# The latent adaLN sums of a diffusion block: three engines' shares against one chain on VectorE

## The chip, the core and the metric

The program runs on one core of one Trainium2 chip. A core has five engines that work side by side, each through its own instructions in order: TensorE (PE in the profile, with its weight loads as PEld), VectorE (DVE), ScalarE (ACT), GpSimd (POOL) and SyncE (SP), which here issues nearly all transfers from HBM. The metric is the device time of one execution in microseconds; less is better. The time before is 1447.01 us, the median of three runs (1440.1 to 1449.32).

## The reference, cut to what matters

One transformer block for 256 latent tokens (width 2048) and 256 context tokens: adaLN, neighbourhood attention with 16 heads, output projection, ConvFFN.

```python
sh1, sc1, g1, sh2, sc2, g2 = adaln(cond_lat, w_ada[i], b_ada[i])    # silu(c) @ w + b, split in six
h = modulate(rms_norm(x, norm_mix_g[i]), sh1, sc1)
csh1, csc1, ... = adaln(cond_ctx, w_ada[i], b_ada[i])
hc = modulate(rms_norm(ctx, norm_mix_g[i]), csh1, csc1)
y, yc = neighbourhood_attention(h, hc, ...)                         # w_qkv, softmax over 256+256 keys, w_o
x = x + g1 * y
hf = modulate(rms_norm(x, norm_ffn_g[i]), sh2, sc2)
x = x + g2 * conv_ffn(hf, ...)
```

The change touches one piece of this: the latent vectors g1, sh2, sc2 and g2. Each is a product of one vector of 2048 values with a 2048 x 2048 part of `w_ada`, thus 2048 x 2048 weights read for 2048 results.

## The kernel before, in words

**Stages.** The products with `w_qkv` come in twelve groups of 512 output columns. For head group 0 (k) and head groups 0 and 1 (v) they are computed at the start, piece by piece, while the first part of adaLN (shift and scale of the mixer) comes in. Then, for each group of four heads (groups 0 to 3), `project` computes the next products: with four token tiles of 128 for k and v (`nt` = 4, latent and context tokens), with two for q (`nt` = 2). In order of time these are q0; k, q of group 1; v, k, q of group 2; k, q, v of group 3. Between the matmuls of such a product the attention of the group before is woven in. Then come the output projection (`w_o`, five rounds in the table `WO`), a norm, the ConvFFN with `w_up` (22 products) and `w_down` (5).

**The split of weights.** Each product is made of three fp32r products of high and low parts. For each weight tile pair (256 x 512 values, 512 KB) SyncE loads `wr`, ScalarE writes the high part `wh` (line 155), VectorE the low part `wl` (line 156). There are four `wr` slots, three of `wh` and two of `wl`, and `ahead` issues two pairs ahead.

**The latent adaLN sums.** `ada_tasks` (lines 252 to 301) makes one column of 512 results out of eight tiles `wa` (each two k of 128 x 512 values); there are 12 columns ahead of the FFN (g1, then sh2, then gs2) and 4 in it (g2). Every k is one step: multiply by the value of the condition that belongs to the row, and add to `acc`. Of the eight parts of a column, three (q = 0, 3, 6) are a chain of multiply-adds on VectorE (lines 274 and 279); the other five are multiplied on ScalarE in place (line 276) and added on GpSimd (line 277) to a second accumulator, whose first step is on VectorE. `finish` adds the two accumulators on VectorE (line 285), transposes on TensorE (line 288), reduces (line 291) and adds the bias (line 294). There are three slots of `wa` (`WA`), and each part starts with the issue of a load two parts ahead, which waits until the part before has let go of its slot.

**What sets the order.** The program is written as one stream of instructions, and a scheduler sets the order on each engine from it. The stream is paced by credits: `ada.tick(r)` adds r, and each whole credit takes one part off the queue. Before, `project` adds 0.44 x `nt` for each weight pair: 1.76 parts with four token tiles, 0.88 with two; in the output projection it is one part for each weight pair, in the FFN 0.25. Attention is paced in the same way by `side.tick`, once for each token tile in `nat` (line 381).

**The normalisation chain.** At the end of a head group, q and k are normalised and transposed (`norm_transpose`, line 515): ScalarE squares (521), VectorE scales (522), GpSimd takes a power (195), VectorE does a Newton step in three instructions of 128 x 4 values (196, 197, 200) and a multiply (526), TensorE transposes (532), ScalarE and VectorE split the result (534, 535). The attention of the next group waits for it.

Of the kernel before, what the change touches and what calls it, by code (L numbers as in the profile page):

```python
# [9 lines left out]
F32 = mybir.dt.float32  # L10
# [5 lines left out]
P = 128  # L16
# [9 lines left out]
CH = 512  # L26
# [3 lines left out]

WA = 3
EPS = 1e-6
# [18 lines left out]
def block_kernel(  # L51
# [200 lines left out]
    def ada_tasks(pool, i, c, dst, gcol=None):  # L252
# [3 lines left out]


        st = {}
# [4 lines left out]
        def part(q):  # L263
            w, pool_ = st[q], q % 3 != 0
            if q < 2:
                st["acc", pool_] = pool.tile(
                    [P, CH], F32, tag=f"acc{pool_}", name="acc", bufs=2 - pool_
                )
            acc = st["acc", pool_]
            for k in range(KT):  # L270
                s = sT[:, q * KT + k, 0:1]
                first = q < 2 and k == 0
                if first:
                    nc.vector.tensor_scalar_mul(acc, w[:, k, :], s)
                elif pool_:
                    nc.scalar.mul(w[:, k, :], w[:, k, :], s)  # L276
                    nc.gpsimd.tensor_add(acc, acc, w[:, k, :])  # L277
                else:
                    nc.vector.scalar_tensor_tensor(  # L279
                        out=acc, in0=w[:, k, :], scalar=s, in1=acc, op0=ALU.mult, op1=ALU.add  # L280
                    )

        def finish():
            acc = st["acc", 0]
            nc.vector.tensor_add(acc, acc, st["acc", 1])
            sp = ms()
# [83 lines left out]
    def nat(psl, tt0, w, kt0, n, first, last):  # L370

        wh, wl = w
        for i, pt in enumerate(psl):
            ts = slice((tt0 + i) * P, (tt0 + i + 1) * P)
            for k in range(n):
# [4 lines left out]
                nc.tensor.matmul(pt, hl(kt, ts), wh[:, k, :], start=False, stop=z)  # L380
            side.tick(side.rate)

    def project(c0, nt):
        psl = [pj() for _ in range(nt)]
        for kt in range(0, KD, KT):
            nat(psl, 0, weight(w_qkv, kt, KT, c0, CH), kt, KT, kt == 0, kt == KD - KT)
            ada.tick(0.44 * nt)
        return psl
# [278 lines left out]

    cols = [ada_tasks(ap, 2, c, g1T) for c in range(4)]
    cols += [ada_tasks(ap, 3, c, sh2T) for c in range(4)]
    cols += [ada_tasks(ap, 4, c, gs2T, S_GF) for c in range(4)]  # L670
    ada.extend(ada_pieces(cols))

# [90 lines left out]
    for i, pieces in enumerate(WO):  # L763
# [5 lines left out]
        for c, cn, k_lo, k_hi in pieces:  # L769
            tick = (lambda: side.tick(cn / 340)) if i == 0 else (lambda: ada.tick(1.0))  # L770
            proj(w_o, NH, c, cn, omv, tick, k_lo, k_hi, pts[c], fold)
# [187 lines left out]
```

## Time and profile before

| | |
|---|---|
| time, median of 3 | 1447.01 us |
| profiled execution: its time, its span | 1445.85 us, 1444.0 us |
| TensorE busy | 1399.1 us (97%) |
| VectorE, ScalarE, GpSimd busy | 1000.0, 778.5, 281.1 us |
| adds on GpSimd (line 277) | 144, 1553 ns on average |
| scalings on ScalarE (line 276) | 144, 718 ns on average |
| multiply-adds on VectorE (line 279) | 80, 921 ns on average |

The span is from the first to the last instruction; 1.85 us of the profiled execution's time lie outside of it. PE is nearly always busy, so time can be found only where PE waits, where its clock was granted at less than full speed, or where an engine beside it begins to make it wait. The profile shows each of these by stage.

### The profile page before, as it was taken

What the parts mean: (1) busy time and instruction counts of PE and PEld (TensorE: products, weight loads), DVE (VectorE), ACT (ScalarE), POOL (GpSimd) and SP (SyncE); (2) the same over time, 40 slices, a digit from 0 to 9 for tenths busy, and PEclk for the clock granted to TensorE, in tenths of its full rate; (3) what the DMA queues carried; (4) which work ended last, traced back from release to release, by engine and by line L of the source; (5) the groups of instructions that cost most, each with busy time, mean ns of one, the idle gap of its engine ahead of it and who ended that gap; (6) DMA issues with size and microseconds to landing.
All of it is one profiled execution on the core that took longest, in us unless ns stands there. A gap on an engine that the chain in (4) does not pass through costs nothing.

```text
span 1444.0 us, 21091 instructions
## 1 busy us (share of the span) xinstructions
PE 1399.1 (97%) x7608; PEld 1167.8 (81%) x7608; DVE 1000.0 (69%) x1541; ACT 778.5 (54%) x1356; POOL 281.1 (19%) x208
## 2 busy tenths in 40 slices
PE   5999999999999999999899999999999999999998
PEld 2666787877787887888788888888888888888888
DVE  4556687686868768756768787887877775545454
ACT  4322265775555675755556566665666654333333
POOL 1000025465445555300101111111111000000000
PEclk9999999999999999999899999999999999999999
DMA  9999548687677677545567777777776666566554
GB/s 308 357 333 313 190 125 269 206 259 218 214 219 254 215 239 232 178 138 189 174 201 224 237 230 242 236 229 234 228 240 196 182 175 206 182 207 204 172 173 156
DMA packets 208920, 317.14 MB, mean 220 GB/s; under 512 B 23360, under 2 KB 87744, under 8 KB 208816
## 3 DMA queue, kind: packets, MB, share of 16 engines
q1 hardware_dynamic: 208688, 315.79, 70.4%
q8 instruction: 59, 0.97, 0.3%
q14 instruction: 45, 0.37, 0.1%
q10 hardware_dynamic: 128, 0.01, 0.0%
HBM read 312.75 MB, written 3.01 MB: 219 GB/s over the span
## 4 chain that ended last, share of the span: by engine, by line
PE 74%; issue 9%; DMA 5%; DVE 4%; ACT 3%; POOL 2%; SPq 1%; DVEq 0%; POOLq 0%; ACTq 0%
PE pj L727 18%; PE pj L733 9%; PE mx L727 8%; PE ms L727 7%; PE pj L379 5%; PE pj L378 5%; PE pj L380 5%; PE mx L733 4%; PE ms L733 4%; DMA wa<-in_w_ada 3%; PE ms L411 2%; PE mx L378 2%; PE mx L379 2%; PE mx L380 2%; POOL acc L277 2%
## 5 line engine op out<-in xcount | busy, mean ns | idle before, releaser
L156 DVE TENSOR_TENSOR wl<-wr,wh 128x1024 fp32r<-128x1024 f32 (+2 forms) x425 | 503.8, 1186 | 280.6 <-PE pj L733 106.3
L155 ACT CAST wh<-wr 128x1024 fp32r<-128x1024 f32 (+2 forms) x425 | 412.1, 971 | 428.8 <-PE pj L727 135.1
L277 POOL TENSOR_TENSOR acc<-acc,wa 128x512 f32<-128x512 f32 x144 | 223.6, 1553 | 428.8 <-issue 260.1
L379 PE MATMUL pj<-wl,hh 128*128 128x512 f32 x512 | 204.7, 400 | 3.5 <-DVE wl L156 3.4
L380 PE MATMUL pj<-wh,hl 128*128 128x512 f32 x512 | 201.7, 397 | 0.0
L378 PE MATMUL pj<-wh,hh 128*128 128x512 f32 x512 | 194.4, 400 | 2.5 <-ACT hh L450 2.5
L727 PE MATMUL pj<-hf,wh 128*128 128x512 f32 x688 | 176.3, 396 | 2.0 <-DVE hf L819 2.0
L727 PEld LDWEIGHTS pj<-hf,wh 128*128 128x128 f32 x688 | 124.9, 191 | 25.1 <-DVE hf L819 2.8
L276 ACT ACTIVATE wa<-wa,sT 128x512 f32<-128x512 f32 x144 | 97.4, 718 | 74.5 <-DMA wa<-in_w_ada 69.3
L379 PEld LDWEIGHTS pj<-wl,hh 128*128 128x128 f32 x512 | 97.7, 191 | 27.2 <-DVE wl L156 6.3
L378 PEld LDWEIGHTS pj<-wh,hh 128*128 128x128 f32 x512 | 96.8, 190 | 26.9 <-issue 3.4
L380 PEld LDWEIGHTS pj<-wh,hl 128*128 128x128 f32 x512 | 97.5, 191 | 19.5
L733 PEld LDWEIGHTS pj<-hf,wl 128*128 128x128 f32 x688 | 94.6, 192 | 6.8
L733 PE MATMUL pj<-hf,wl 128*128 128x256 f32 x688 | 97.8, 285 | 0.0
L727 PE MATMUL mx<-hf,wh 128*128 128x512 f32 x352 | 97.7, 394 | 0.0
L727 PE MATMUL ms<-hf,wh 128*128 128x512 f32 x336 | 90.9, 390 | 0.0
L279 DVE SCALAR_TENSOR_TENSOR acc<-wa,sT,acc 128x512 f32<-128x512 f32 x80 | 73.7, 921 | 6.9 <-DMA wa<-in_w_ada 6.3
L727 PEld LDWEIGHTS ms<-hf,wh 128*128 128x128 f32 x336 | 63.1, 188 | 14.2
L727 PEld LDWEIGHTS mx<-hf,wh 128*128 128x128 f32 x352 | 60.6, 190 | 7.8
L478 DVE TENSOR_TENSOR vsum<-vsum,mx 128x512 f32<-128x512 f32 x64 | 43.2, 684 | 34.2 <-PE mx L380 34.0
L733 PEld LDWEIGHTS mx<-hf,wl 128*128 128x128 f32 x352 | 53.7, 189 | 7.1 <-DVE wl L156 0.4
L584 POOL TENSOR_TENSOR bt<-bt,maskt 128x384 f32<-128x384 f32 x16 | 17.9, 1123 | 206.4 <-DMA bt<-rpd 173.7
(251 smaller groups left out, 2212.0 us busy)
## 6 DMA issues: line engine op xcount, KB each, us to landing
wr<-in_w_up SPq DMA_DIRECT2D x160, 512.0 KB, 4.5
wa<-in_w_ada SPq DMA_DIRECT2D x128, 512.0 KB, 4.6
wr<-in_w_qkv SPq DMA_DIRECT2D x93, 512.0 KB, 4.8
wr<-in_w_down SPq DMA_DIRECT2D x63, 512.0 KB, 4.8
wx<-in_w_ada SPq DMA_DIRECT2D x56, 512.0 KB, 8.6
wr<-in_w_o SPq DMA_DIRECT2D x24, 512.0 KB, 3.9
wr<-in_w_down SPq DMA_DIRECT2D x45, 256.0 KB, 3.0
wr<-in_w_up SPq DMA_DIRECT2D x16, 384.0 KB, 3.4
```

The source lines that it names most:

```text
L155: a = nc.scalar.copy(hi[:, :kn, :cn], w[:, :kn, :cn])
L156: b = nc.vector.tensor_tensor(out=lo[:, :kn, :cn], in0=w[:, :kn, :cn], in1=hi[:, :kn, :cn].bitcast(F32), op=ALU.subtract,)
L276: nc.scalar.mul(w[:, k, :], w[:, k, :], s)
L277: nc.gpsimd.tensor_add(acc, acc, w[:, k, :])
L279: nc.vector.scalar_tensor_tensor(out=acc, in0=w[:, k, :], scalar=s, in1=acc, op0=ALU.mult, op1=ALU.add)
L378: nc.tensor.matmul(pt, hh[:, kt, ts], wh[:, k, :], start=a, stop=False)
L379: nc.tensor.matmul(pt, hh[:, kt, ts], wl[:, k, :], start=False, stop=False)
L380: nc.tensor.matmul(pt, hl(kt, ts), wh[:, k, :], start=False, stop=z)
L411: nc.tensor.matmul(ap_[32 * k : 32 * k + 32, :n], s32[:, 4 * q + k, :], w[:, k * n : (k + 1) * n], start=(q == 0), stop=(q == 3), tile_pos ...
L478: nc.vector.tensor_add(acc[:, h0 + i, :], acc[:, h0 + i, :], pr_[i])
L727: nc.tensor.matmul(pts[b][:, : t1 - t0], wh[:, k, bs], mov(kt, slice(t0, t1)), start=(kt == 0 and t0 == 0), stop=False,)
L733: nc.tensor.matmul(pts[b][:, :T], wl[:, k, bs], mov(kt, slice(0, T)), start=False, stop=(kt == kn - 1),)
```

## The change

Every part of a column becomes a chain on VectorE: one multiply, then 15 multiply-adds into one accumulator. The scalings on ScalarE, the additions on GpSimd, the second accumulator and the addition in `finish` go. `wa` gets a fourth slot, so that loads are issued three parts ahead. The pace is set for each token tile in `nat` in place of each weight pair: 0.5 with four token tiles and 0.1 with two, thus 2.0 and 0.2 parts for each weight pair (before 1.76 and 0.88). In the output projection it is 0.6 for each weight pair (before 1.0), in the FFN 0.25 as before. The columns of gs2 now come ahead of those of sh2.

```diff
--- before.py
+++ after.py
@@ -28,7 +28,9 @@
 
 RATE, RATE3 = 0.46, 0.36
 
-WA = 3
+ADA_RATE = {2: 0.1, 4: 0.5}
+
+WA = 4
 EPS = 1e-6
 NEG = -1e30
 
@@ -254,35 +256,27 @@
         st = {}
 
         def load(q):
             st[q] = wload(w_ada, q * KT, KT, i * D + c * CH, CH, pool)
 
         def part(q):
-            w, pool_ = st[q], q % 3 != 0
-            if q < 2:
-                st["acc", pool_] = pool.tile(
-                    [P, CH], F32, tag=f"acc{pool_}", name="acc", bufs=2 - pool_
-                )
-            acc = st["acc", pool_]
+            w = st[q]
+            if q == 0:
+                st["acc"] = pool.tile([P, CH], F32, tag="acc", name="acc", bufs=2)
+            acc = st["acc"]
             for k in range(KT):
                 s = sT[:, q * KT + k, 0:1]
-                first = q < 2 and k == 0
-                if first:
+                if q == 0 and k == 0:
                     nc.vector.tensor_scalar_mul(acc, w[:, k, :], s)
-                elif pool_:
-                    nc.scalar.mul(w[:, k, :], w[:, k, :], s)
-                    nc.gpsimd.tensor_add(acc, acc, w[:, k, :])
                 else:
                     nc.vector.scalar_tensor_tensor(
                         out=acc, in0=w[:, k, :], scalar=s, in1=acc, op0=ALU.mult, op1=ALU.add
                     )
 
         def finish():
-            acc = st["acc", 0]
-            nc.vector.tensor_add(acc, acc, st["acc", 1])
+            acc = st["acc"]
             sp = ms()
             for b in range(4):
                 nc.tensor.transpose(sp[:, b * P : (b + 1) * P], acc[:, b * P : (b + 1) * P], ident)
@@ -379,12 +373,14 @@
                 nc.tensor.matmul(pt, hh[:, kt, ts], wl[:, k, :], start=False, stop=False)
                 nc.tensor.matmul(pt, hl(kt, ts), wh[:, k, :], start=False, stop=z)
             side.tick(side.rate)
+            ada.tick(ada.rate)
 
     def project(c0, nt):
         psl = [pj() for _ in range(nt)]
+        ada.rate = ADA_RATE[nt]
         for kt in range(0, KD, KT):
             nat(psl, 0, weight(w_qkv, kt, KT, c0, CH), kt, KT, kt == 0, kt == KD - KT)
-            ada.tick(0.44 * nt)
+        ada.rate = 0.0
         return psl
 
 
@@ -666,8 +662,8 @@
         return [seq + w[0] + s[2] + w[1] + t[2] + s[3] + w[2] + t[3] + w[3]]
 
     cols = [ada_tasks(ap, 2, c, g1T) for c in range(4)]
+    cols += [ada_tasks(ap, 4, c, gs2T, S_GF) for c in range(4)]
     cols += [ada_tasks(ap, 3, c, sh2T) for c in range(4)]
-    cols += [ada_tasks(ap, 4, c, gs2T, S_GF) for c in range(4)]
     ada.extend(ada_pieces(cols))
 
     v, v1 = [[split_v([vsums[g][:, tt, :] for tt in range(4)], g)] for g in range(2)]
@@ -767,7 +763,7 @@
         elif i > 1:
             pts = {c: [bank() for _ in range(cn // P)] for c, cn, _, _ in pieces}
         for c, cn, k_lo, k_hi in pieces:
-            tick = (lambda: side.tick(cn / 340)) if i == 0 else (lambda: ada.tick(1.0))
+            tick = (lambda: side.tick(cn / 340)) if i == 0 else (lambda: ada.tick(0.6))
             proj(w_o, NH, c, cn, omv, tick, k_lo, k_hi, pts[c], fold)
         if i == 0:
             side.drain()
```

In the changed kernel's rows below, lines have moved: 156 is 158, 279 is 274, 274 is 272, 291 is 285, 196, 197 and 200 are 198, 199 and 202, 522 and 526 are 518 and 522, 788 is 784.

The first place is VectorE's order in the product for k of head group 2 (the groups are 0 to 3; four token tiles), over two weight pairs. `acc` and `wa` are the adaLN sums, `wl` the low part of a weight pair, `rs` and `ptl` belong to attention. Before:

```order
L156 TENSOR_TENSOR wl<-wr,wh 128x1024
L279 SCALAR_TENSOR_TENSOR acc<-wa,sT,acc 128x512
L623 RECIPROCAL rs<-rs 128x1
L291 TENSOR_REDUCE sh2T<-ms 128x4
L279 SCALAR_TENSOR_TENSOR acc<-wa,sT,acc 128x512
L294 TENSOR_TENSOR sh2T<-sh2T,sm 128x4
L156 TENSOR_TENSOR wl<-wr,wh 128x1024
L279 SCALAR_TENSOR_TENSOR acc<-wa,sT,acc 128x512 x2
L636 TENSOR_TENSOR ptl<-ms,pth 128x4x128 x2
L285 TENSOR_TENSOR acc<-acc 128x512
```

And now:

```order
L158 TENSOR_TENSOR wl<-wr,wh 128x1024
L274 SCALAR_TENSOR_TENSOR acc<-wa,sT,acc 128x512
L619 RECIPROCAL rs<-rs 128x1
L274 SCALAR_TENSOR_TENSOR acc<-wa,sT,acc 128x512
L619 RECIPROCAL rs<-rs 128x1
L274 SCALAR_TENSOR_TENSOR acc<-wa,sT,acc 128x512 x2
L285 TENSOR_REDUCE g1T<-ms 128x4
L288 TENSOR_TENSOR g1T<-g1T,sm 128x4
L158 TENSOR_TENSOR wl<-wr,wh 128x1024
L274 SCALAR_TENSOR_TENSOR acc<-wa,sT,acc 128x512
L272 TENSOR_SCALAR acc<-wa,sT 128x512
L274 SCALAR_TENSOR_TENSOR acc<-wa,sT,acc 128x512 x2
```

Each weight pair now has four steps of the sums where it had two; over the eight pairs of this product they are 32 where they were 12.

The second place is VectorE's order in the product for q that follows (two token tiles), where the normalisation chains of the group's end lie (`ss`, `nt`, `nr`, `qn`). Before:

```order
L156 TENSOR_TENSOR wl<-wr,wh 128x1024
L274 TENSOR_SCALAR acc<-wa,sT 128x512
L526 TENSOR_TENSOR qn<-oT,nr 128x512
L522 TENSOR_SCALAR ss<-ss 128x4
L279 SCALAR_TENSOR_TENSOR acc<-wa,sT,acc 128x512
L291 TENSOR_REDUCE sh2T<-ms 128x4
L156 TENSOR_TENSOR wl<-wr,wh 128x1024
L274 TENSOR_SCALAR acc<-wa,sT 128x512
L196 TENSOR_TENSOR nt<-nr 128x4
L294 TENSOR_TENSOR sh2T<-sh2T,sm 128x4
L522 TENSOR_SCALAR ss<-ss 128x4
L197 SCALAR_TENSOR_TENSOR nt<-nt,ss 128x4
```

And now:

```order
L158 TENSOR_TENSOR wl<-wr,wh 128x1024
L202 SCALAR_TENSOR_TENSOR nr<-nt,nr 128x4
L198 TENSOR_TENSOR nt<-nr 128x4
L522 TENSOR_TENSOR qn<-oT,nr 128x512
L199 SCALAR_TENSOR_TENSOR nt<-nt,ss 128x4
L202 SCALAR_TENSOR_TENSOR nr<-nt,nr 128x4
L522 TENSOR_TENSOR qn<-oT,nr 128x512
L158 TENSOR_TENSOR wl<-wr,wh 128x1024
L518 TENSOR_SCALAR ss<-ss 128x4
L158 TENSOR_TENSOR wl<-wr,wh 128x1024
L198 TENSOR_TENSOR nt<-nr 128x4
L199 SCALAR_TENSOR_TENSOR nt<-nt,ss 128x4
```

The steps of the sums that stood between the instructions of the chain are gone from here; over the eight pairs of this product they are 6 where they were 7, and 4 of the 6 stand in the first pair.

The third place is VectorE's order in the fourth round of the output projection, where `sacc` gathers the squares for the norm. Before:

```order
L156 TENSOR_TENSOR wl<-wr,wh 128x1024
L788 TENSOR_TENSOR sacc_5379<-sacc_5379,sq 128x256
L156 TENSOR_TENSOR wl<-wr,wh 128x1024
L788 TENSOR_TENSOR sacc_5379<-sacc_5379,sq 128x256 x2
L156 TENSOR_TENSOR wl<-wr,wh 128x1024 x4
```

And now:

```order
L158 TENSOR_TENSOR wl<-wr,wh 128x1024
L274 SCALAR_TENSOR_TENSOR acc<-wa,sT,acc 128x512
L784 TENSOR_TENSOR sacc_5198<-sacc_5198,sq 128x256
L158 TENSOR_TENSOR wl<-wr,wh 128x1024
L274 SCALAR_TENSOR_TENSOR acc<-wa,sT,acc 128x512
L285 TENSOR_REDUCE sh2T<-ms 128x4
```

About one step of the sums for each weight pair is new here; before, the sums had ended ahead of the output projection.

## The prediction

> **What bounds the kernel now.** The page's first part, and then the view of the stretches: first products end near 195 us, attention with its products runs to 610, the output projection to 705, then a turn and the FFN.
>
> ```profile
> span 1444.0 us, 21091 instructions
> PE 1399.1 (97%) x7608; PEld 1167.8 (81%) x7608; DVE 1000.0 (69%) x1541; ACT 778.5 (54%) x1356; POOL 281.1 (19%) x208
> 195.00:610.00 415.00, 398.85 (x1917) 327.37 (x1916) 314.96 (x481) 262.25 (x548) 207.40 (x143) 0.99 0.72 225
> 610.00:705.00 95.00, 92.76 (x577) 82.50 (x575) 60.44 (x99) 50.14 (x86) 0.00 (x0) 1.00 0.51 165
> 740.00:1130.00 390.00, 390.00 (x2241) 342.83 (x2240) 316.73 (x458) 244.96 (x387) 56.93 (x36) 1.00 0.75 227
> ```
>
> Columns of a stretch: its length, then busy time of PE, PEld, DVE, ACT and POOL, granted clock, DMA share, GB/s. In the FFN stretch PE is busy for all of 390 us although DVE is at 316.73 (81%) and POOL still adds: nothing is to be had there. In the attention stretch PE idles 415 - 398.85 = 16.15 us. That, and time at a lower clock, is all that the change can reach. Some of its products next, one by one:
>
> ```profile
> 376.00:429.00 53.00, 52.45 (x262) 43.77 (x261) 37.14 (x47) 33.27 (x68) 24.76 (x19) 1.00 0.74 226
> 429.00:460.00 31.00, 27.81 (x118) 22.00 (x117) 27.35 (x40) 19.63 (x44) 17.75 (x13) 0.89 0.76 248
> 515.00:543.00 28.00, 28.00 (x146) 23.60 (x145) 21.65 (x35) 20.38 (x57) 13.31 (x10) 1.00 0.79 245
> 543.00:602.00 59.00, 55.28 (x256) 44.81 (x255) 43.35 (x76) 36.53 (x76) 31.17 (x21) 0.97 0.73 224
> ```
>
> The first is the product for k of group 2, the second its q with the normalisation of that group, the third q of group 3, the fourth v of group 3 with its normalisation. PE is full in the first and third (0.55 and 0 us idle) and waits in the second and fourth (3.19 and 3.72 us). The loss sits where the normalisation chains are, not where most of the sums are. These stretches are also those with a clock under 1: (1 - 0.89) x 31 = 3.4 us and (1 - 0.97) x 59 = 1.8 us, together 5.2. Whom PE waits for in 195 to 610 us (us in total, times, longest):
>
> ```profile
> PE pj L379 <- DVE wl L156: 3.4, 4, 1.5
> PE ms L532 <- DVE qn L526: 2.7, 2, 1.5
> PE mx L532 <- DVE qn L526: 2.5, 2, 1.7
> PE mx L645 <- ACT pth L635: 2.1, 1, 2.1
> PE ms L631 <- ACT pr L624: 1.4, 2, 0.8
> PE ms L532 <- ACT kh L534: 1.3, 1, 1.3
> PE ms L532 <- DVE gs2T L291: 0.8, 1, 0.8
> PE pj L727 <- DVE om L566: 0.8, 1, 0.8
> PE ms L648 <- DVE ptl L636: 0.7, 1, 0.7
> ```
>
> Together 15.7 us. What makes DVE and ACT late there? First DVE's groups of this stretch (count, busy us, mean ns), and below the line the same kinds from stretches with little or no work on GpSimd: the first 195 us, and 740 to 1130 us.
>
> ```profile
> L156 DVE TENSOR_TENSOR wl<-wr,wh 128x1024 fp32r<-128x1024 f32 x76 | 106.9, 1407 | 21.0 <-PE pj L379 13.6 <-ACT oT L653 2.9 <-ACT wa L276 1.5
> L279 DVE SCALAR_TENSOR_TENSOR acc<-wa,sT,acc 128x512 f32<-128x512 f32 x60 | 58.7, 979 | 6.8 <-DMA wa<-in_w_ada 6.3
> L274 DVE TENSOR_SCALAR acc<-wa,sT 128x512 f32<-128x512 f32 x24 | 14.2, 596 | 0.0
> L196 DVE TENSOR_TENSOR nt<-nr 128x4 f32<-128x4 f32 x21 | 9.8, 468 | 8.3 <-POOL nr L195 8.3
> L200 DVE SCALAR_TENSOR_TENSOR nr<-nt,nr 128x4 f32<-128x4 f32 x22 | 9.2, 418 | 0.5
> L285 DVE TENSOR_TENSOR acc<-acc 128x512 f32<-128x512 f32 x12 | 8.2, 686 | 4.5 <-POOL acc L277 4.4
> L197 DVE SCALAR_TENSOR_TENSOR nt<-nt,ss 128x4 f32<-128x4 f32 x22 | 6.8, 310 | 0.3
> L294 DVE TENSOR_TENSOR gs2T<-gs2T,sm 128x4 f32<-128x4 f32 x4 | 0.6, 156 | 0.0
> ...
> L156 DVE TENSOR_TENSOR wl<-wr,wh 128x1024 fp32r<-128x1024 f32 x21 | 25.7, 1223 | 20.3 <-PE mx L379 11.6 <-issue 6.0 <-PE pj L379 1.5
> L279 DVE SCALAR_TENSOR_TENSOR acc<-wa,sT,acc 128x512 f32<-128x512 f32 x20 | 14.9, 747 | 0.1
> L274 DVE TENSOR_SCALAR acc<-wa,sT 128x512 f32<-128x512 f32 x8 | 3.8, 481 | 0.0
> ```
>
> The same multiply-add takes 979 ns here and 747 there, the low part 1407 against 1223, and instructions of 128x4 values 310 to 468 where an undisturbed one (L294) takes 156. The order of time at 438 us shows by what; and the second cause is on ACT at 365 us:
>
> ```profile
> 438.22 1.25 DVE L196 TENSOR_TENSOR nt<-nr 128x4 f32<-128x4 f32 x1 [0.31 <-POOL nr L195]
> 439.70 1.14 DVE L200 SCALAR_TENSOR_TENSOR nr<-nt,nr 128x4 f32<-128x4 f32 x1
> 438.17 2.66 POOL L277 TENSOR_TENSOR acc<-acc,wa 128x512 f32<-128x512 f32 x2
> 365.58 0.72 ACT L276 ACTIVATE wa<-wa,sT 128x512 f32<-128x512 f32 x1 [3.97 <-DMA wa<-in_w_ada]
> 366.20 0.57 ACT L635 CAST pth<-ms 128x512 fp32r<-128x512 f32 x1
> ```
>
> Two instructions of the chain last 1.25 and 1.14 us while GpSimd's two adds run beside them. And ScalarE stood 3.97 us before a scaling whose tile had not landed, with attention's copy of `pth` queued behind it: that is PE's longest wait above (2.1 us).
>
> **The change part by part.**
>
> *GpSimd and ScalarE are freed.* The rows that go (the second holds what ACT loses by waiting for tiles):
>
> ```profile
> L277 POOL TENSOR_TENSOR acc<-acc,wa 128x512 f32<-128x512 f32 x108 | 166.7, 1543 | 99.5 <-ACT wa L276 53.3 <-DVE acc L274 17.7 <-ACT wh L155 13.5
> L276 ACT ACTIVATE wa<-wa,sT 128x512 f32<-128x512 f32 x108 | 73.2, 719 | 74.5 <-DMA wa<-in_w_ada 69.3 <-DVE acc L279 1.7 <-POOL acc L277 1.4
> ```
>
> GpSimd keeps 207.4 - 166.7 = 40.7 us (the powers and the bias adds), so about a fifth of its overlap with DVE stays.
>
> *VectorE's work, attention stretch.* Of 192 steps ahead of the FFN, the changed order leaves about 172 here, 11 of them first steps: 161 x 0.747 + 11 x 0.481 = 125.6 us. Out go 58.7 + 14.2 + 8.2 = 81.1. DVE's other instructions get shorter: 76 x (1407 - 1223) = 14.0, 21 x (468 - 156) = 6.6, 22 x (418 - 156) = 5.8, 22 x (310 - 156) = 3.4, together 29.8 us, of which I count four fifths, 23.8. Net +20.7: 315 becomes 336 of 415 us (81%), as full as DVE is in the FFN stretch without one PE wait. So this term is nothing on average. Locally the product for k of group 2 is the tightest: 37.14 us of DVE work, plus 20 more steps (32 for 12) x 0.747 = 14.9, less 8 x 0.184 and 12 x 0.232 of lengthening, 4.3: 47.7 of 53 us (90%). Two `wl` buffers let DVE be late by a weight pair less one split, 53 / 8 - 1.2 = 5.4 us, and a pair's four steps are 3.0. I take 2 us of new short waits over the five products with four token tiles; between 0 and 18 (worked out as a rival).
>
> *VectorE's work, output projection.* About 20 steps, 15 us, join 60.44 us in 95 us: 79%. The rounds' heads, where DVE also updates x1, are denser; no row shows a sum beside them. Nothing at best, and at worst a step of 0.75 us late at each of the rounds two to four and the last transpose, 3 us. I take 1.5.
>
> *VectorE's work, FFN.* 4 x (15 x 0.747 + 0.481) = 46.7 us replace 14.9 + 3.8 + 2.7 (four L285); DVE goes to some 86% less what L156 regains. The cover is PE's full row; 0 us, at worst 2.
>
> *The fourth slot.* A load is now issued when the part four earlier is done, on DVE itself rather than by GpSimd at the end of a handover:
>
> ```profile
> SPq L139 <- POOL acc L277: 103.9, 51, 5.8
> wa<-in_w_ada SPq DMA_DIRECT2D x128, 512.0 KB, 4.6
> ```
>
> Three parts at 53 / 16 = 3.3 us lie between issue and use, less 1.5 us for the slot's last reader: 8.4 us against a landing of 4.6. `wr` loads queued behind on SP gain too. If the cover goes, the wait stands on DVE, with `wl` behind it; ACT's 69.3 us shows how often that was so with three slots. I take 0; bounds: 3 us gained on `wr`, 3 lost.
>
> *PE's waits, one by one.* `qn` (5.2): every chain loses two to three times about 1 us and waits for powers queued behind adds; the longest of four waits is 1.7. All gone: 5.2. `kh` 1.3 and `pth` 2.1 stood behind a scaling: gone. `pr` 1.4: one of two, 0.7. `wl` 3.4: splits under adds, and queues behind them; four fifths, 2.7. `ptl`, `om`, `gs2T` stay. Sum: 12.0; bounds 6 and 15.7.
>
> *The clock.* The stretches under 1 are those with bunched waits. If it follows them, most of 5.2 us comes back; I take 4.5; bounds 0 and 5.2.
>
> Sum: -12.0 - 4.5 + 2 + 1.5 = -13.0, and another 1 us of waits for weights on PEld that go with the same causes: -14. Against the profiled execution's own 1445.85 us this gives **1432 us**; that execution lies 1.2 us under the median of the three, which is within their spread.
>
> **The rivals.**
>
> *Half of it returns (same).* The chain's waits go, but DVE's bursts of four steps, 3.0 us, stand in front of `qn`, `ptl` and the max of the scores, which in order cannot pass. Six chains lie at each of four group ends; if a third of the 24 waits for one pair of steps, 1.5 us, 12 us are given back, and with the clock's share and the rest about 1441 is left. For: in-order DVE at 90% in the products with four tiles. Against: in the order shown for q of group 2 no step stands between the chain's instructions any more, and at 515 to 543 us PE waits nowhere with DVE at 77%.
>
> *DVE becomes the bound (slower).* Place: the five products with four token tiles. If the steps keep their 979 ns and the splits their 1407 (the cause not being the adds), the product for k of group 2 needs 37.14 + 20 x 0.979 = 56.7 us of DVE in 53: 3.7 late, five times 18.5; nothing comes back, and 1445.85 + 18.5 = 1464 us. It decides from a mean of (53 - 37.14) / 20 = 0.79 us for each added step. Against: 747 in the FFN, next to 36 adds still, and 128x4 instructions that lengthen just where an add runs. The Trainium skill (Trace Analysis, section Optimizing Scalar/DVE Operations) speaks for this rival: it says that offloading from DVE to ScalarE or even GpSimd may make sense where DVE is saturated, and the change takes such offloading back. By that rule the time would be this rival's; the trace has DVE at 76% in the stretch, so the rule's condition isn't met on average.
>
> *The clock stays.* The half clock at 429 to 460 us comes with waits of at most 1.5 us each. If it is set by something other than these waits, 4.5 us of the gain is missing: 1436 or 1437. The Trainium skill (TensorE: Matmul & The Clock Gate, section Part 1) has the clock fall to half after one idle window of about 3.4 us; no wait here is as long, so by its letter these stretches would not be explained by them, and the gain would be this rival's. The trace's bunching of the clock with the waits speaks for the other reading.
>
> **How the numbers follow.** Chances: forecast 0.62 (1421 to 1438), half returns 0.22 (1441), the clock alone stays 0.08 (1436.5), DVE the bound 0.08 (1464). A measurement of this kernel tells about 1% from no change, 14.5 us, so "faster" means under 1432.5, in the middle of the forecast's own range. Of its 0.62 I put 0.50 under that, since the profile's rows count only waits of PE that show, and a stretch without them (515 to 543) has none at all. Faster 0.50; same 0.12 + 0.22 + 0.08 = 0.42 and a little of the last; slower 0.07. Range: at the low end all waits and the clock, 1445.85 - 16.15 - 5.2 = 1424.5, and 3 for the spread of runs; at the high end the second case with its 3 to 4 us of uncertain `wr` and FFN terms: 1421 to 1445.
>
> **What would show it.** Right: no POOL rows but powers, bias adds and the FFN's products; L156 near 1.23 us and the multiply-add near 0.75 throughout; the 128x4 instructions near 0.16; no `qn` among PE's waits; ACT with no wait for `wa`; PE idle in the attention stretch under 6 us, granted clock 1.00 to 705 us. Wrong: PE waits for `wl` in the products with four token tiles (the second rival), waits at the transposes in spite of short instructions (the first), or DVE waiting for `wa` (the fourth slot not enough).

## The result, and the profile after

The changed kernel takes **1420.2 us** (median of four runs, 1419.36 to 1422.49); the kernel before, beside it, 1446.15 us (1440.1 to 1449.32). The ratio is 0.9826, with a 95% interval of 0.9803 to 0.985: about 26 us less, where the prediction had 14.

The page of the changed kernel, its first lines:

```profile
span 1417.6 us, 20783 instructions
PE 1386.8 (98%) x7608; PEld 1164.8 (82%) x7608; DVE 1022.4 (72%) x1669; ACT 694.9 (49%) x1212; POOL 59.9 (4%) x64
```

The span fell by 26.4 us with the same 7608 matmuls. VectorE has 22 us more work, ScalarE 84 less, GpSimd 221 less. To see where the time came from, take the same work in both kernels: from the end of the first products to the end of the fourth round of the output projection. The view of the stretches (length, then busy time and count of PE, PEld, DVE, ACT and POOL, granted clock, DMA share, GB/s), first of before:

```profile
195.00:692.00 497.00, 480.08 (x2396) 398.54 (x2395) 365.69 (x562) 304.66 (x617) 207.40 (x143) 0.99 0.68 214
```

And of the changed kernel, the same stretch, then the products for v and k of group 2, q of group 2 and v of group 3, and the FFN:

```profile
195.00:666.00 471.00, 469.60 (x2396) 396.34 (x2395) 390.39 (x658) 242.69 (x509) 43.10 (x35) 1.00 0.72 224
308.00:363.00 55.00, 55.00 (x273) 46.12 (x272) 50.32 (x90) 26.38 (x61) 6.81 (x5) 1.00 0.82 254
363.00:416.00 53.00, 53.00 (x267) 44.56 (x267) 42.04 (x68) 22.23 (x48) 5.19 (x5) 1.00 0.77 235
416.00:440.00 24.00, 24.00 (x115) 19.99 (x114) 18.12 (x32) 14.87 (x38) 2.78 (x3) 1.00 0.69 211
523.00:578.00 55.00, 54.23 (x264) 44.83 (x263) 50.10 (x87) 27.20 (x63) 4.89 (x4) 1.00 0.87 276
714.00:1104.00 390.00, 390.00 (x2241) 343.01 (x2240) 314.98 (x491) 223.97 (x352) 0.00 (x0) 1.00 0.74 226
```

Both have 2396 matmuls there, one in 497 us and the other in 471: all of the gain lies here. PE's idle time fell from 497 - 480.08 = 16.9 us to 1.4. Its busy time fell as well, by 10.5 us, although the matmuls are the same. The half clock is gone from this stretch, which gives back 5.1 us at most: it was granted for 6.8 and 3.4 us before. The rest is not that single matmuls got shorter: away from the half clock those of the products last 393 to 395 ns before (195 to 448 us) and 392 to 394 ns after (195 to 440 us). But 2396 matmuls in 469.6 us of busy time are one every 196 ns, so their records lie over one another, and a matmul whose weights come a little late makes the busy time longer without showing idle time. That this is the rest of the 10.5 us is inferred, not measured. The product for q of group 2, with its normalisation, went from 31 us to 24. The FFN is as it was.

VectorE's groups in the changed kernel, 195 to 585 us (count, busy us, mean ns, idle time before them):

```profile
L274 DVE SCALAR_TENSOR_TENSOR acc<-wa,sT,acc 128x512 f32<-128x512 f32 x161 | 124.2, 774 | 1.8
L158 DVE TENSOR_TENSOR wl<-wr,wh 128x1024 fp32r<-128x1024 f32 x76 | 93.4, 1230 | 30.1 <-PE pj L373 21.1 <-issue 5.9 <-PE mx L373 1.1
...
L202 DVE SCALAR_TENSOR_TENSOR nr<-nt,nr 128x4 f32<-128x4 f32 x22 | 4.2, 191 | 0.4
L199 DVE SCALAR_TENSOR_TENSOR nt<-nt,ss 128x4 f32<-128x4 f32 x22 | 3.5, 158 | 0.3
L198 DVE TENSOR_TENSOR nt<-nr 128x4 f32<-128x4 f32 x21 | 3.3, 158 | 3.6 <-POOL nr L197 3.3
```

The multiply-add went from 979 to 774 ns, the low part from 1407 to 1230, the three instructions of the Newton step from 468, 310 and 418 to 158, 158 and 191. In order of time, one chain of group 2, which before had instructions of 1.25 and 1.14 us:

```profile
422.63 0.15 DVE L198 TENSOR_TENSOR nt<-nr 128x4 f32<-128x4 f32 x1
422.82 0.16 DVE L199 SCALAR_TENSOR_TENSOR nt<-nt,ss 128x4 f32<-128x4 f32 x1
423.02 0.16 DVE L202 SCALAR_TENSOR_TENSOR nr<-nt,nr 128x4 f32<-128x4 f32 x1
```

Now the waits once more, but of the weight loads (PEld) in place of the matmuls (us in total, times, longest). Before, 195 to 692 us, the first five of 17 rows and the last:

```profile
PEld pj L379 <- DVE wl L156: 5.8, 8, 1.7
PEld mx L532 <- DVE qn L526: 3.4, 3, 2.1
PEld ms L631 <- ACT pr L624: 2.9, 4, 1.3
PEld mx L645 <- ACT pth L635: 2.3, 1, 2.3
PEld pj L727 <- DVE om L566: 1.9, 2, 1.1
...
PEld pj L378 <- ACT oT L681: 0.2, 1, 0.2
```

And after, 195 to 666 us, all rows:

```profile
PEld ms L729 <- DVE wl L158: 1.0, 2, 0.8
PEld pj L723 <- DVE om L562: 1.0, 1, 1.0
PEld pj L373 <- DVE wl L158: 0.4, 1, 0.4
PEld ms L645 <- DVE vv L555: 0.2, 1, 0.2
```

The 17 rows of before sum to 26.7 us, those of after to 2.6. On PE's own row the waits of the same stretch were 16.5 us. A weight load that waits while the last matmul still runs shows on PEld in full and on PE only in part. Neither row is the truth: of the 26 us, at most 5 belong to the half clock, so 21 or more are waits, between PE's 15.5 and PEld's 24.1.

### The profile page after: what moved, and what is told of

Read it like the earlier page. It is cut to its first block, busy times and chain, and to the rows that moved or that the text cites. A ratio compares the mean times of both kernels' runs of the same rounds, so it can differ in the third digit from the quotient of the medians.

```text
span 1417.6 us, 20783 instructions
## 1 busy us (share of the span) xinstructions
PE 1386.8 (98%) x7608; PEld 1164.8 (82%) x7608; DVE 1022.4 (72%) x1669; ACT 694.9 (49%) x1212; POOL 59.9 (4%) x64
## 4 chain that ended last, share of the span: by engine, by line
PE 94%; DMA 2%; DVE 2%; SPq 1%; ACT 1%; issue 1%; POOL 0%; DVEq 0%; ACTq 0%; POOLq 0%
PE pj L723 20%; PE pj L729 10%; PE mx L723 10%; PE pj L372 8%; PE pj L373 8%; PE pj L374 8%; PE ms L723 7%; PE mx L729 5%; PE ms L729 4%; PE mx L372 2%; PE mx L373 2%; PE ms L407 2%; PE mx L374 2%; DMA wx<-in_w_ada 1%; PE ms L627 1%; SPq L401 1%
## 5 line engine op out<-in xcount | busy, mean ns | idle before, releaser
L158 DVE TENSOR_TENSOR wl<-wr,wh 128x1024 fp32r<-128x1024 f32 (+2 forms) x425 | 478.1, 1126 | 284.8 <-PE pj L729 102.3
L274 DVE SCALAR_TENSOR_TENSOR acc<-wa,sT,acc 128x512 f32<-128x512 f32 x240 | 183.2, 765 | 2.5
L372 PEld LDWEIGHTS pj<-wh,hh 128*128 128x128 f32 x512 | 95.7, 188 | 26.4 <-issue 3.4
L729 PE MATMUL mx<-hf,wl 128*128 128x256 f32 x352 | 55.9, 282 | 0.0
L729 PE MATMUL ms<-hf,wl 128*128 128x256 f32 x336 | 54.7, 283 | 0.0
L407 PE MATMUL ms<-wx,s 128*32 128x512 f32 (+1 forms) x288 | 36.9, 582 | 16.3 <-DMA wx<-in_w_ada 16.3
```

What stands on the lines that cost most here:

```text
L158: b = nc.vector.tensor_tensor(out=lo[:, :kn, :cn], in0=w[:, :kn, :cn], in1=hi[:, :kn, :cn].bitcast(F32), op=ALU.subtract,)
L274: nc.vector.scalar_tensor_tensor(out=acc, in0=w[:, k, :], scalar=s, in1=acc, op0=ALU.mult, op1=ALU.add)
L372: nc.tensor.matmul(pt, hh[:, kt, ts], wh[:, k, :], start=a, stop=False)
L407: nc.tensor.matmul(ap_[32 * k : 32 * k + 32, :n], s32[:, 4 * q + k, :], w[:, k * n : (k + 1) * n], start=(q == 0), stop=(q == 3), tile_pos ...
L729: nc.tensor.matmul(pts[b][:, :T], wl[:, k, bs], mov(kt, slice(0, T)), start=False, stop=(kt == kn - 1),)
```

## The experiments

The change has four parts: the chain on VectorE (which takes work from ScalarE and from GpSimd), the fourth slot, the pace, and the order of columns. Theory A: the time comes from the work that goes, above all from GpSimd's adds, since these lengthen VectorE's instructions while they run. Theory B: it comes from the pace and the order, which keep the sums out of the products with two token tiles.

### Pace and order alone

The split over three engines and the three slots of before, with the new pace and order. Against the changed kernel:

```diff
-WA = 4
+WA = 3
...
-            w = st[q]
...
+            w, pool_ = st[q], q % 3 != 0
...
+            acc = st["acc", pool_]
...
+                elif pool_:
+                    nc.scalar.mul(w[:, k, :], w[:, k, :], s)
+                    nc.gpsimd.tensor_add(acc, acc, w[:, k, :])
...
+            nc.vector.tensor_add(acc, acc, st["acc", 1])
```

> The kernel before (sums on three engines, three slots) with the new pace and column order alone. Theory A (GpSimd's adds lengthen VectorE's instructions and ScalarE's scalings wait for tiles; the pace does little): most of the 26 us stay lost, 1436 to 1444 us, 128x4 instructions of the normalisation still over 0.3 us on average, PE waits for qn or pth. Theory B (the gain is the pace: no steps between the chain's instructions in the q products): 1420 to 1428 us with the lengthened instructions still there.

Measured: 1441.2 us, ratio 0.9956 [0.9939, 0.9973]. Stretch and two of VectorE's groups, 195 to 610 us:

```profile
195.00:610.00 415.00, 400.09 (x1943) 329.38 (x1942) 307.70 (x472) 259.70 (x546) 182.75 (x132) 1.00 0.70 218
...
L280 DVE SCALAR_TENSOR_TENSOR acc<-wa,sT,acc 128x512 f32<-128x512 f32 x53 | 47.8, 902 | 6.9 <-DMA wa<-in_w_ada 6.3
L198 DVE TENSOR_TENSOR nt<-nr 128x4 f32<-128x4 f32 x21 | 14.0, 667 | 10.9 <-POOL nr L197 10.9
```

The instructions stay as long as they were, the chain's first even longer (667 ns), and PE still idles 14.9 us. Pace and order by themselves are worth some 6 us. What they change in the trace is mostly the half clock, of which 3.4 us are left at the end of this stretch (10.2 before).

### The chain with the old pace and order

The reverse: chain and fourth slot, with before's pace and order.

```diff
-            ada.tick(ada.rate)
...
-        ada.rate = ADA_RATE[nt]
...
+            ada.tick(0.44 * nt)
...
+    cols += [ada_tasks(ap, 3, c, sh2T) for c in range(4)]
     cols += [ada_tasks(ap, 4, c, gs2T, S_GF) for c in range(4)]
-    cols += [ada_tasks(ap, 3, c, sh2T) for c in range(4)]
...
-            tick = (lambda: side.tick(cn / 340)) if i == 0 else (lambda: ada.tick(0.6))
+            tick = (lambda: side.tick(cn / 340)) if i == 0 else (lambda: ada.tick(1.0))
```

> The changed kernel (one chain on VectorE, four slots) with the old pace and column order. Theory A: the waits caused by GpSimd and ScalarE are gone, 1420 to 1427 us. Theory B: the q products now carry 14 steps where the changed kernel has 6; VectorE's work in the q product of group 2 is then 0.81 x 23.8 + 8 x 0.75 = 25.3 us in 23.8, the normalisation waits, PE loses 3 to 6 us in each of four q products: 1432 to 1444 us.

Measured: 1422.86 us, ratio 0.9829 [0.9803, 0.9854].

```profile
195.00:610.00 415.00, 413.75 (x2066) 346.97 (x2066) 350.60 (x602) 214.25 (x465) 47.01 (x35) 1.00 0.74 231
```

This is the whole gain, within the interval. PE idles 1.25 us although VectorE has 350.60 us of work in the stretch (84%; the changed kernel has 341.47). Theory B falls: with the chain, pace and order add nothing that can be measured, so their 6 us of the run above are best read as part of the same loss.

### Three slots

```diff
-WA = 4
+WA = 3
```

> The changed kernel with three slots of wa in place of four. If the fourth slot carries part of the gain: loads are issued two parts ahead, 2 x 3.3 - 1.5 = 5.1 us against a landing of 4.8, VectorE waits for tiles with wl behind it, 1424 to 1432 us. If it doesn't: 1419 to 1423 us and no wait of VectorE for wa over 3 us in all.

Measured: 1422.79 us, ratio 0.9838 [0.9814, 0.9862]. VectorE's waits for `wa` in its chain, 195 to 610 us:

```profile
DVE acc L274 <- DMA wa<-in_w_ada: 2.4, 2, 1.9
```

With four slots only one wait for `wa`, of 0.8 us, is left on VectorE. By the medians the slot is worth 2.6 us, and the intervals overlap. The following kernels with added work on GpSimd have three slots, and are held against this one.

### Only ScalarE's share back

The five parts are scaled on ScalarE in place again, and added on VectorE; one accumulator, four slots.

```diff
+                elif q % 3 != 0:
+                    nc.scalar.mul(w[:, k, :], w[:, k, :], s)
+                    nc.vector.tensor_add(acc, acc, w[:, k, :])
```

> The changed kernel with the scalings of five parts in eight back on ScalarE (in place, waiting for the tile as before), their adds on VectorE, GpSimd without adds: ScalarE's share of the split alone. If ScalarE's waits for tiles were a cause of their own: ACT waits for wa again, PE waits for pth, pr or wh, 1426 to 1436 us. If the cause was GpSimd alone (its late handing back of the slots made the tiles late as well): 1419 to 1424 us.

Measured: 1430.28 us, ratio 0.9887 [0.9865, 0.9908], 10 us over the changed kernel. ScalarE's row over the whole span, and two of PE's waits of 195 to 700 us that grew:

```profile
L274 ACT ACTIVATE wa<-wa,sT 128x512 f32<-128x512 f32 x160 | 106.9, 717 | 47.1 <-DMA wa<-in_w_ada 36.4 <-DVE acc L275 5.0 <-DVE wl L158 3.2
...
PE pj L726 <- DVE om L565: 3.7, 2, 3.2
PE ms L647 <- DVE ptl L635: 1.5, 1, 1.5
```

No instruction of VectorE is longer (its low part is at 1244 ns), but ScalarE stands 36.4 us before tiles that have not landed, with attention's copies behind it in order, even with four slots. In this form ScalarE's share costs some 10 us. How much of that is ScalarE's standing is not shown. PE's waits that grew are for `om` and `ptl`, which VectorE writes, and VectorE has a wait here that it didn't have before: it stands 3.4 us before adds whose scaled values ScalarE hasn't finished (before, GpSimd did that waiting). And the first 195 us, ahead of any latent sum, lose about 1.4 us: 875 matmuls in place of 882, at some 0.2 us each.

### Only GpSimd's share back

Adds on GpSimd with a second accumulator, their scalings on VectorE; three slots, new pace.

```diff
-WA = 4
+WA = 3
...
+            acc = st["acc", pool_]
...
+                elif pool_:
+                    nc.vector.tensor_scalar_mul(w[:, k, :], w[:, k, :], s)
+                    nc.gpsimd.tensor_add(acc, acc, w[:, k, :])
...
+            nc.vector.tensor_add(acc, acc, st["acc", 1])
```

> The changed kernel (new pace, three slots, two accumulators) with the adds of five parts in eight back on GpSimd and their scalings on VectorE: GpSimd's share alone, ScalarE out of it. Theory A, lock: multiply-adds over 0.85 us, 128x4 instructions 0.25 to 0.45 us on average, PE waits for qn or wl, 1432 to 1445 us. If ScalarE in the middle was the cause: 1419 to 1426 us.

Measured: 1446.47 us, ratio 0.9994 [0.9982, 1.0007]: as slow as before, 24 us over the kernel with three slots. VectorE's groups, 195 to 610 us:

```profile
L158 DVE TENSOR_TENSOR wl<-wr,wh 128x1024 fp32r<-128x1024 f32 x76 | 98.2, 1293 | 12.6 <-PE pj L380 7.4 <-issue 2.5 <-ACT wh L157 1.5
L280 DVE SCALAR_TENSOR_TENSOR acc<-wa,sT,acc 128x512 f32<-128x512 f32 x53 | 61.8, 1166 | 2.1 <-DMA wa<-in_w_ada 1.7
```

The multiply-add is at 1166 ns with ScalarE out of the matter. Here VectorE scales as well, which is more work for it, so the run alone doesn't part the adds' hold from VectorE's load. The next ones do. The two shares' prices, 10 and 24 us, do not add up: together, with the new pace, they cost 21 (1441.2 - 1420.2).

### Adds that nobody waits for

The changed kernel with three slots, and 144 adds on GpSimd on a tile of zeros beside it. The sums are complete, the adds are extra work without a result.

```diff
-WA = 4
+WA = 3
...
+            if q % 3 != 0:
+                for k in range(KT - (q == 1)):
+                    nc.gpsimd.tensor_add(idle, idle, idle)
```

> The changed kernel with three slots, and beside it the 144 adds of 128x512 values on GpSimd as before, but on a tile of zeros that nothing waits for: only GpSimd's hold on VectorE comes back. Theory A, lock alone: multiply-adds at 0.95 us and 128x4 instructions at 0.3 to 0.45 us on average again, waits for qn and wl return, 8 to 16 us over the kernel with three slots; with VectorE then beyond the product's length in the k and v products (37 + 20 x 0.98 = 56.7 us in 53) up to 30 us. If the gain came from ScalarE and the transfers: within 3 us of the kernel with three slots, even with lengthened instructions.

Measured: 1464.04 us, ratio 1.0118 [1.0095, 1.014]. It is a miss in its place: with nothing to wait for, most adds ran in the first 195 us (POOL 131.00 us busy there). The stretch of this kernel, and of before:

```profile
0.00:195.00 195.00, 153.90 (x735) 92.11 (x736) 133.77 (x192) 53.77 (x87) 131.00 (x124) 0.94 0.82 257
```
```profile
0.00:195.00 195.00, 177.07 (x882) 114.58 (x883) 111.37 (x233) 65.91 (x125) 10.14 (x21) 0.99 0.89 284
```

Even so it says something: work that nothing depends on costs 41 us against the kernel with three slots. PE gets through 735 matmuls in place of 882, and VectorE is busy longer with fewer instructions: its 16 multiply-adds of 128x256 on `xl` there last 957 ns on average, where they last 482 ns in the kernel before. To learn about the stretch in question, the adds have to be tied to it.

### The same adds at the old times

Each part of a column that had adds makes a small copy on VectorE (`tok`, one value a partition), from which two adds on GpSimd start (one in the part q = 1); the sums don't use them. 97 of the 144 adds then lie in 195 to 610 us, where the kernel before had 108.

```diff
+                if k == 0 and q % 3 != 0:
+                    tok = pool.tile([P, 1], F32, tag="tok", name="tok", bufs=4)
+                    nc.vector.tensor_copy(tok, acc[:, 0:1])
+                    for _ in range(KT - (q == 1)):
+                        nc.gpsimd.tensor_add(idle, idle, tok.to_broadcast([P, CH]))
```

> The changed kernel with three slots, and GpSimd adding 128x512 values beside the sums at the times of the old adds, on a tile that nobody needs: each waits for a one-column copy on VectorE (80 in all, about 0.1 us each), and nothing waits for GpSimd but its own powers and bias adds. Theory A, lock alone, in the attention stretch: multiply-adds 0.9 us or more, PE idle there 10 us or more, 1432 to 1450 us. If the lengthening is hidden and only the dependence on GpSimd's adds hurt: 1422 to 1426 us.

Measured: 1454.13 us, ratio 1.0045 [1.0027, 1.0064]. Stretch and groups of 195 to 590 us, the adds over the whole span, and two of PE's waits of 195 to 700 us:

```profile
195.00:590.00 395.00, 380.11 (x1822) 310.15 (x1821) 358.91 (x569) 185.35 (x414) 171.12 (x124) 1.00 0.71 214
...
L276 DVE SCALAR_TENSOR_TENSOR acc<-wa,sT,acc 128x512 f32<-128x512 f32 x152 | 140.0, 923 | 3.8 <-DMA wa<-in_w_ada 1.9
L198 DVE TENSOR_TENSOR nt<-nr 128x4 f32<-128x4 f32 x22 | 10.2, 462 | 10.6 <-POOL nr L197 10.4
...
L283 POOL TENSOR_TENSOR idle<-idle,tok 128x512 f32<-128x512 f32 x144 | 215.0, 1493 | 509.9 <-DVE tok L281 499.6 <-DVE rs L626 3.5 <-DVE gs2T L295 1.7
...
PE mx L535 <- DVE qn L529: 4.0, 3, 2.0
PE pj L380 <- DVE wl L158: 4.0, 4, 1.5
```

The signature of before is back: 923 ns, 462 ns (before 979 and 468), waits for `qn` and `wl`, and 14.9 us of idle PE.

### The ties without the adds

The same kernel without its last two lines, so that only the small copies are left.

```diff
-                    for _ in range(KT - (q == 1)):
-                        nc.gpsimd.tensor_add(idle, idle, tok.to_broadcast([P, CH]))
```

> The run with tied adds, without the adds: three slots and the 80 one-column copies on VectorE alone (0.15 us each, 8 us in the attention stretch). If the 31 us of the tied adds are GpSimd's: 1422 to 1426 us, multiply-adds at 0.77 us, PE idle in the attention stretch under 3 us. If the copies in VectorE's chain are what cost: over 1435 us.

Measured: 1425.93 us, ratio 0.9834 [0.98, 0.9868]. Groups of 195 to 590 us:

```profile
L276 DVE SCALAR_TENSOR_TENSOR acc<-wa,sT,acc 128x512 f32<-128x512 f32 x161 | 123.9, 771 | 3.9 <-DMA wa<-in_w_ada 2.3
...
L198 DVE TENSOR_TENSOR nt<-nr 128x4 f32<-128x4 f32 x21 | 3.3, 158 | 6.4 <-POOL nr L197 6.4
```

The copies cost nothing that can be measured (0.9838 without them). So 1454.13 - 1425.93 = 28 us are the adds' doing alone, and nobody waits for their result: what hurts is that they run. (The two kernels ran on different chips; by their ratios to the kernel before it is 31 us.) Running, they can hurt in two ways: they lengthen VectorE's instructions, and GpSimd's own powers queue behind them. VectorE waits 10.4 us for powers with the adds and 6.4 us without, so the queue looks like the smaller part; the runs don't part the two further.

### Writes in place of adds

The same ties, with GpSimd filling the tile (a memset of 128x512) in place of adding. There are two tiles in turn, and the tie on VectorE is an add of one column that reads the tile to be filled, in place of the copy.

```diff
-                    nc.vector.tensor_copy(tok, acc[:, 0:1])
+                    nc.vector.tensor_add(tok, acc[:, 0:1], zs[0][:, 0:1])
...
-                        nc.gpsimd.tensor_add(idle, idle, tok.to_broadcast([P, CH]))
+                        nc.gpsimd.memset(zs[0], 0.0)
+                    zs.reverse()
```

> As the run with tied adds, but GpSimd writes zeros (128x512, 144 times, at the times of the old adds, on two tiles in turn) and reads nothing. If VectorE's two-input instructions are held by a read port that GpSimd's adds occupy: multiply-adds stay near 0.77 us and the time within 5 us of the run with the copies alone, 1422 to 1430 us. If any work on GpSimd holds VectorE: multiply-adds of 0.9 us or more, 1435 us or more.

Measured: 1425.63 us, ratio 0.9833 [0.9796, 0.9871]. The multiply-add of 195 to 590 us and the fills of the whole span:

```profile
L277 DVE SCALAR_TENSOR_TENSOR acc<-wa,sT,acc 128x512 f32<-128x512 f32 x161 | 123.9, 771 | 2.2 <-DMA wa<-in_w_ada 0.5
...
L284 POOL MEMSET idle<- 128x512 f32 x144 | 75.6, 526 | 594.8 <-DVE tok L282 591.3
```

771 ns, to the nanosecond that of the kernel without any of it. Work on GpSimd that only writes does not lengthen VectorE here; adds that read do. The Trainium skill (SBUF — State Buffer, section Who interferes with whom) states just this: a VectorE instruction with two inputs in SBUF contends with a GpSimd instruction that reads SBUF, not with one that only writes. The runs agree, 771 against 923 ns. One reserve: a fill lasts 526 ns and an add 1493, so the fills also overlap less.

### Adds of half the size

```diff
-                        nc.gpsimd.tensor_add(idle, idle, tok.to_broadcast([P, CH]))
+                        nc.gpsimd.tensor_add(idle[:, : CH // 2], idle[:, : CH // 2], tok.to_broadcast([P, CH // 2]))
```

> The run with tied adds, each add on 256 in place of 512 values: half of the cost alone. If PE's loss goes with the time that GpSimd holds VectorE: a multiply-add of 0.82 to 0.88 us and between a quarter and a half of the 31 us, 1430 to 1438 us. If it goes with the number of adds: as with 512 values, 1450 us or more. If a short hold is hidden: 1422 to 1427 us.

Measured: 1427.98 us, ratio 0.9847 [0.9805, 0.9888], not to be told from the ties alone, and below what was expected. Stretch and multiply-add, 195 to 590 us, and the adds of the whole span; and in the second block the stretch of the ties alone:

```profile
195.00:590.00 395.00, 390.23 (x1902) 325.42 (x1902) 346.84 (x606) 198.16 (x438) 143.78 (x132) 0.99 0.74 227
...
L276 DVE SCALAR_TENSOR_TENSOR acc<-wa,sT,acc 128x512 f32<-128x512 f32 x161 | 133.2, 829 | 4.6 <-DMA wa<-in_w_ada 3.0
...
L283 POOL TENSOR_TENSOR idle<-idle,tok 128x256 f32<-128x256 f32 x144 | 154.4, 1072 | 537.4 <-DVE tok L281 524.6 <-DVE rs L626 6.0 <-DVE gs2T L295 1.7
```
```profile
195.00:590.00 395.00, 392.62 (x1929) 327.81 (x1928) 329.55 (x611) 202.34 (x445) 40.91 (x35) 1.00 0.74 228
```

GpSimd works 154.4 us, 72% of the full adds' 215.0, and the multiply-add is lengthened by 58 ns, 38% of the 152; the time grows by 2 us, 7% of the 28. In the profiled stretch the loss is larger than by the times: 1902 matmuls where the ties alone have 1929 and the full adds 1822, thus 27 fewer against 107, a quarter. Either way it is less than in proportion to the lengthening. VectorE's average load doesn't say why: it works 347 us of 395 here and 359 with the full adds, but the kernel before had it at 315 of 415 and PE idled 16.2 us. What differs as well is the first instruction of the Newton step, 315 ns here and 462 with the full adds. The run also weakens the reserve on the fills: their 75.6 us, half of these adds' time, lengthened nothing at all, where half of 58 ns would be plain to see.

### A faster pace

Does VectorE become the bound when the steps are packed closer? Four token tiles at 0.8 in place of 0.5, thus 6.4 steps for each weight pair.

```diff
-ADA_RATE = {2: 0.1, 4: 0.5}
+ADA_RATE = {2: 0.1, 4: 0.8}
```

> The changed kernel with a pace of 0.8 in place of 0.5 for each token tile in the k and v products: 3.2 parts, 6.4 steps for each weight pair, so that VectorE has 37.1 - 12 x 0.98 + 51 x 0.76 = 64 us of work in a product of 53. The price of the rival that VectorE becomes the bound: the sums end two products earlier, and until then each of about three products with four token tiles loses 5 to 11 us: 1434 to 1450 us, PE waiting for wl. If the steps slip behind and VectorE has slack elsewhere: 1420 to 1425 us.

Measured: 1431.79 us, ratio 0.9891 [0.9868, 0.9914], 11.6 us over the changed kernel and less than was expected. PE's two longest waits and VectorE's wait for tiles, 195 to 590 us:

```profile
PE mx L528 <- DVE nt L199: 3.8, 1, 3.8
PE pj L373 <- DVE wl L158: 3.2, 6, 1.1
...
DVE acc L272 <- DMA wa<-in_w_ada: 12.7, 8, 2.8
```

Now PE waits for `wl`, and the tiles come late on VectorE itself, with everything queued behind. This comes near the rival "VectorE becomes the bound", and the pace of the change stays short of it. But VectorE is not full: it stands 12.7 us before tiles and works 328.63 of 395 us. The transfers are the brake, so what a full VectorE would cost stays untested.

### The old order of columns

```diff
-    cols += [ada_tasks(ap, 4, c, gs2T, S_GF) for c in range(4)]
     cols += [ada_tasks(ap, 3, c, sh2T) for c in range(4)]
+    cols += [ada_tasks(ap, 4, c, gs2T, S_GF) for c in range(4)]
```

> The changed kernel with sh2 ahead of gs2 again, as in the kernel before. The last of the columns end in the output projection's fourth round, and the products with gs2 stand in its second: their writer would come up to 45 us after its first reader was due; ScalarE and the squares for the norm wait, banks come free later. If that holds PE: 1425 to 1440 us with PE waits between 585 and 690 us. If only side work moves: 1419 to 1423 us.

Measured: 1420.75 us, ratio 0.9797 [0.9764, 0.983], beside 0.9826 [0.9803, 0.985] of the change: the same within the intervals. The order of sh2 and gs2 changes nothing that these runs can tell. No kernel here is measurably better than the changed one.

## Why the prediction was right and wrong

**The mechanism: right, and shown for GpSimd's adds.** The sum rested on VectorE's instructions being lengthened by them. The durations taken from rows with little work on GpSimd came true (low part 1223 forecast, 1230 measured; multiply-add 747 and 774; 128x4 instructions 156 and 158 to 191), and the tied adds brought the old ones back, at 28 us. The second cause, ScalarE standing before tiles, was read from the trace: its 69.3 us of such waits are gone, and with them PE's 4.8 us of waits for ScalarE (`pth`, `pr`, `kh`), of which the prediction counted 4.1. The run with its share alone costs 10 us, but brings new waits on VectorE, so the size of this cause stays open.

**VectorE's work: right on average, and for the places nearly so.** Forecast were 336 of 415 us (81%) in the attention stretch; the same work, 195 to 585 us after the change, takes 326.92 of 390 us (84%), 9 us less than forecast. The tightest product was to be k of group 2 at 90%; it is v of group 2, 50.32 of 55 us (91%), with k at 79%. PE waits at neither.

**The step that failed: the size of the waits.** The forecast was -14, and the stretch measured -26. By its terms:

| term | forecast | measured |
|---|---|---|
| PE's idle time: waits that go | -12.0 | |
| PE's idle time: new short waits (2 + 1.5) | +3.5 | |
| PE's idle time, together | -8.5 | -15.5 |
| weight loads, inside PE's busy time | -1.0 | -5.4 |
| the clock | -4.5 | -5.1 |
| sum | -14.0 | -26.0 |

(The clock's 5.1 is a bound, half of the 10.2 us that were at half the clock; the prediction had 5.2 from rounded shares. The 5.4 is the rest of the 10.5 us of busy time.) Of the 12 us that were missed, 7.0 are in the first three rows. I had kept 3.7 us of waits in the attention stretch (`ptl`, `om`, `gs2T` and remainders); of these only `om` is left, with 0.8 us on PE's row. `ptl` belonged to the same cause as the rest: with the tied adds it came back, with 3.0, 2.1 and 2.1 us at three places. And I had added 3.5 us of new waits for a fuller VectorE, of which PE's row shows 0.6, for `wl` in the output projection. Another 4.4 us are the weight loads. "Another 1 us" was a guess where a row was to be had: PEld's waits were 26.7 us in this stretch, 10 over PE's own. So the sentence that PE's idle time and its lower clock are "all that the change can reach" does not hold: 5.4 us more lay inside the busy time.

**The rivals.** "Half of it returns" did not occur: bursts of three or four steps stand before the splits and PE hardly waits for them. "VectorE becomes the bound" was to decide at a mean of 0.79 us for an added step; the mean is 0.774, nearly there, yet nothing happens at 91%. The price of 18.5 us counted each microsecond of overload as lost; the run with the faster pace lost 11.6, with the transfers as the brake, so no run shows that price. The Trainium skill's advice to move work off VectorE (Perfetto Trace Analysis, section Optimizing Scalar/DVE Operations), which stood for this rival, is for a saturated VectorE; here it worked 76% of the stretch, and bringing work back to it gained 26 us. The same passage of the Trainium skill warns that moving work between GpSimd and VectorE might not help, since they share a read port, and the runs agree with that: the adds alone cost 28 us. "The clock stays" fell: no half clock is left ahead of the turn into the FFN.

**The output projection, the FFN, the slot.** The 1.5 us for the projection did not come. In the FFN PE is busy for 390.00 of 390 us as before, and VectorE's 314.98 us there are below its 316.73 of before: its longer sums (60 multiply-adds for 20) are paid by instructions that no add lengthens any more, such as the splits, 1308 ns there before and 1222 now. (The prediction's 86% for VectorE there is 88% by its own terms; with the shorter splits it became 81%.) The slot, taken at 0, is worth 0 to 2.6.

**The range.** Its low end was PE's whole idle row and the clock, less 3 us for the spread: 1421. The time is 1420.2, just under it. An upper bound on a gain that is read from PE's row alone isn't one.

## What to carry to other kernels

Before handing VectorE's work to GpSimd, look at how long VectorE's own two-input instructions last while GpSimd reads; the smallest ones on a chain suffer most. VectorE's average load doesn't tell whether that costs time: the kernel before idled 16.2 us in the attention stretch with VectorE at 76%, the chain with the old pace 1.3 us at 84%. Size waits for TensorE's operands from the weight loads' row as well as from the matmuls': the gain lay between the two. And an engine that attention or a normalisation waits for in order should not hold instructions that wait for a transfer.

## What the runs showed of the hardware that was not expected

**The half clock without a long wait.** Before, about 450 us. In order of time, PE's two waits (in brackets), and then the stretch:

```profile
449.64 0.63 PE L532 MATMUL ms<-ident,qn 128*128 128x128 f32 x4 [1.14 <-DVE qn L526]
451.76 0.79 PE L379 MATMUL pj<-wl,hh 128*128 128x512 f32 x1 [1.50 <-DVE wl L156]
...
448.00:458.00 10.00, 7.36 (x22) 5.38 (x21) 8.48 (x11) 4.42 (x6) 4.36 (x3) 0.66 0.81 255
```

A granted clock of 0.66 over 10 us is 6.8 us at half speed. By slices of one microsecond it falls at 451.1 us, inside the second wait. In the 3.41 us before that PE was busy for 1.40 us (41%), and in the 3.41 us before the other fall of the attention stretch, at 553.5 us, for 1.34 us (39%). The Trainium skill (TensorE: Matmul & The Clock Gate, section Part 1) has the half clock after an idle window of about 3.4 us; neither of the two waits here is half as long. In the attention stretch it is seen in kernels with bunched waits (before, pace alone, each share alone, idle, full and half adds, the faster pace), and not in the changed kernel, the chain with the old pace, three slots, the ties alone, the fills or the old order of columns. The half clock lasts 3.41 us or a multiple of it in all these kernels (but for the last one, which the end of the trace cuts off). With time cut by that step, from 195 to 660 us, ten falls of the clock follow a piece in which PE was busy for 13 to 49%, and one (with the idle adds) a piece of 56%; of the pieces that no fall follows, the lowest has 50%. So short waits that add up to about half of such a piece are enough here. At the turn into the FFN falls follow pieces of up to 71%; what makes the difference there stays open.

**Reading, not writing, is what lengthens.** 144 adds of 128x512 took the multiply-add from 771 to 923 ns and cost 28 us; 144 fills of the same size, each a third as long, left it at 771 and cost nothing. The expectation had left open which it would be.
